# Rotary embedding on one core: tile 3's load moves from SyncE's queue to GpSimd's and waits for tile 1's arithmetic

## The chip, the core and the metric

One core of one Trainium2 chip. The metric is the device time of one execution in microseconds (us), as the median of several runs. Engines that matter here: VectorE (DVE), which does all the arithmetic; SyncE (SP) and GpSimd (POOL), which issue transfers from their queues; and the core's 16 DMA engines, which carry the transfers out. TensorE and ScalarE are not used.

## The reference

Half of each head's 64 elements are rotated in pairs by position, the other half is passed through:

```python
batch, seq, heads, dim = (16, 512, 16, 64)
x1, x2 = x[..., :32], x[..., 32:]
rotated_first  = x1[..., :16] * cos[..., :16] - x1[..., 16:] * sin[..., :16]
rotated_second = x1[..., :16] * sin[..., :16] + x1[..., 16:] * cos[..., :16]
out = concatenate([rotated_first, rotated_second, x2], axis=-1)   # float32
```

`x` has 16 x 512 x 16 x 64 float32 numbers, 33.55 MB, and the output has as many. `cos` and `sin` (512 x 32) are small; their first 16 columns are used.

## The kernel before

The 8192 rows of `x` (batch and position; one row is 16 heads of 64, 4 KB) are cut into four tiles, t = 0 to 3. A tile has 128 partitions with 16 consecutive rows each: 64 KB on a partition, 8.39 MB in all. The tiles lie in `ring`, which has three slots (`NS = 3`), so tile 3 uses tile 0's slot again. Work is in place: a tile is loaded into its slot, half of each head is rotated there, and the whole slot is stored from there. So tile 3 can be loaded only when tile 0 has been stored.

`load` (line 56) and `store` (line 59) each issue one DMA for the rows lo to hi of a tile. `rotate` (lines 91 to 112) does a tile or a part of one with four kinds of instruction on VectorE: two multiplications (lines 97 and 98, the first into a PSUM buffer `b_t`, the second in place), a subtraction (line 99) and an addition (line 106). It returns the subtraction and the list of additions, so that a transfer can be tied to one of them. `hold` (lines 114 to 122) ties it: the transfer is issued only after that instruction has ended. The framework adds the waits that the data need by itself: a load into a used slot waits for the landing of that slot's stores, a store waits for the arithmetic on its rows, and the arithmetic waits for its load's landing.

The table of cosines and sines is made first (lines 62 to 89): two small DMAs from GpSimd's queue (lines 64 and 65) and some copies on VectorE. Tiles 0 and 1 and the upper half of tile 2 are loaded meanwhile (lines 66 to 68).

The main part (lines 124 to 141) gives the order of issue on each queue. Each queue works its own list in order, and an entry that waits holds up what is behind it:

- SP: loads of tile 0, tile 1 and the upper half of tile 2; the two stores of tile 0 (lines 126 and 127; the first is held until the third quarter of tile 0 is done); load of the lower half of tile 2 (line 128); load of tile 3 (line 129); store of tile 1 (line 132, held by line 138 until the subtraction of rows 0 to 4 of tile 2); store of tile 3 (line 141).
- POOL: the two table loads, then the store of tile 2 (line 136).
- DVE: tile 0 in two halves, tile 1 in two halves, tile 2's upper half, then its rows 0 to 4, then 5 to 7, then tile 3 in two halves.

Of the kernel before, what the change touches and what calls it, by code (L numbers as in the profile page):

```python
# [1 line left out]

# [4 lines left out]


@with_exitstack
def kernel(  # L10
    ctx: ExitStack,
    tc: tile.TileContext,
    x: bass.AP,
    cos: bass.AP,
    sin: bass.AP,
    out: bass.AP,
):
    nc = tc.nc
    fp32 = mybir.dt.float32
    P = 128  # L20
    B, S, H, D = x.shape
    Q = D // 4
    HF = D // 2

    K = 16
    T = B * S // (P * K)
    PB = S // K
    REP = P // PB  # L30
    R = H * D
    NS = 3
    KC = K // 2
    KM = 5
    KP = K - 4

    xf = x.rearrange("b s h d -> (b s h d)").rearrange("(t p f) -> t p f", t=T, p=P)
    of = out.rearrange("b s h d -> (b s h d)").rearrange("(t p f) -> t p f", t=T, p=P)
    cosf = cos.rearrange("(p k) j -> p (k j)", k=K)
    sinf = sin.rearrange("(p k) j -> p (k j)", k=K)  # L40

    const_pool = ctx.enter_context(tc.tile_pool(name="const", bufs=1))
    b_pool = ctx.enter_context(tc.tile_pool(name="bp", bufs=1, space=bass.MemoryType.PSUM))


    ring = const_pool.tile([P, NS, K, H, D], fp32)
    stage = const_pool.tile([P, 2, K, HF], fp32)
    spun = const_pool.tile([P, 2 * K, Q], fp32)
    packed = const_pool.tile([PB, 2 * K, Q], fp32)
    table = const_pool.tile([P, 2, K, 2, Q], fp32)  # L50

    def rows(t, lo, hi):
        return ring[:, t % NS, lo:hi].rearrange("p k h d -> p (k h d)")

    def load(t, lo=0, hi=K):
        return nc.sync.dma_start(out=rows(t, lo, hi), in_=xf[t, :, lo * R : hi * R])

    def store(t, lo=0, hi=K, queue=nc.sync):
        return queue.dma_start(out=of[t, :, lo * R : hi * R], in_=rows(t, lo, hi))  # L59


    nc.vector.memset(stage[:, :, :, 0:Q], 0.0)  # L62
    spread = stage.rearrange("(j b) t k i -> j b t (k i)", b=REP)
    nc.gpsimd.dma_start(out=spread[:, 0, 0], in_=cosf)  # L64
    nc.gpsimd.dma_start(out=spread[:, 0, 1], in_=sinf)  # L65
    load(0)
    load(1)
    load(2, KC, K)

    PQ = PB // REP
    nc.vector.stream_shuffle(  # L74
        out=spun[:],
        in_=stage.rearrange("p t k j -> p (t k) j")[:, :, 0:Q],
        mask=[j % PQ * REP for j in range(PB)],
    )
    for q in reversed(range(REP)):
        n = PQ * (q + 1)  # L80
        nc.vector.tensor_copy(out=packed[0:n], in_=spun[q * PB : q * PB + n])  # L81

    for r in range(REP):
        nc.vector.tensor_copy(  # L84
            out=table[r * PB : (r + 1) * PB].rearrange("p t k c j -> p (t k) c j"),
            in_=packed.unsqueeze(2).to_broadcast((PB, 2 * K, 2, Q)),
        )
    C = table[:, 0].rearrange("p k c j -> p k (c j)")
    Sn = table[:, 1].rearrange("p k c j -> p k (c j)")

    def rotate(t, lo, hi, cut=None):
        x1 = ring[:, t % NS, lo:hi, :, 0:HF]
        c = C[:, lo:hi].unsqueeze(2).to_broadcast((P, hi - lo, H, HF))
        s = Sn[:, lo:hi].unsqueeze(2).to_broadcast((P, hi - lo, H, HF))
        b_full = b_pool.tile([P, KC, H, HF], fp32, name="b_t")
        b_t = b_full[:, 0 : hi - lo]
        nc.vector.tensor_mul(out=b_t, in0=x1, in1=s)  # L97
        nc.vector.tensor_mul(out=x1, in0=x1, in1=c)  # L98
        first = nc.vector.tensor_sub(  # L99
            out=x1[:, :, :, 0:Q], in0=x1[:, :, :, 0:Q], in1=b_t[:, :, :, Q:HF]  # L100
        )
        ends = [hi - lo] if cut is None else [cut - lo, hi - lo]
        done = []
        for a, b in zip([0] + ends, ends):
            done.append(
                nc.vector.tensor_add(  # L106
                    out=x1[:, a:b, :, Q:HF],
                    in0=x1[:, a:b, :, Q:HF],
                    in1=b_t[:, a:b, :, 0:Q],
                )  # L110
            )
        return first, done

    def hold(transfer, point):
        tc.add_manual_dep(
            transfer.ins,
            point.ins.name,
            mybir.DependencyInfo(
                mybir.DependencyClass.Sync, mybir.DependencyReason.DATA
            ),  # L120
            reason="the store follows the loads at the DMA engines",
        )

    rotate(0, 0, KC)
    _, close = rotate(0, KC, K, cut=KP)
    hold(store(0, 0, KC), close[0])
    store(0, KC, K)
    load(2, 0, KC)
    load(3)
    rotate(1, 0, KC)  # L130
    rotate(1, KC, K)
    behind_loads = store(1)
    rotate(2, KC, K)
    near, _ = rotate(2, 0, KM)
    rotate(2, KM, KC)
    store(2, queue=nc.gpsimd)

    hold(behind_loads, near)
    rotate(3, 0, KC)
    rotate(3, KC, K)  # L140
    store(3)


# [1 line left out]
_INS = ['x', 'cos', 'sin']  # L145
_OUTS = [((16, 512, 16, 64), 'float32')]


# [23 lines left out]
```

## Time and profile before

| what | us |
|---|---|
| median of 3 runs (lowest to highest) | 161.62 (161.36 to 161.76) |
| the profiled execution's own time | 161.67 |
| its span (first to last instruction of the program) | 159.8 |
| VectorE busy | 113.0 (71%) in 48 instructions |
| GpSimd busy | 1.9 (1%) in 7 instructions |
| data moved by the DMA engines | 67.24 MB, 421 GB/s over the span |

The profile counts microseconds from the start of the span; 1.87 us of the profiled execution's time lie outside it. It tells for each engine when its instructions ran and what they waited for. For the DMA engines it has a record of each packet, with its queue, start, duration and size: q1 is SP's queue, q0 is POOL's. A packet of a tile's transfer is one partition's piece, 64 KB for a whole tile and 32 KB for half a tile, and each of the 16 engines carries the pieces of 8 partitions. In its tables over windows of time a packet's whole time and size are booked where the packet starts, so that a window's DMA share can be over 1.

### The profile page before, as it was taken

The page shows a single profiled execution, that of the slowest core. Times are in us where ns is not written, and L with a number is a line of the kernel's source. Part 1 is how long each engine was busy: PE and PEld are TensorE (multiplying, and loading weights), DVE is VectorE, ACT ScalarE, POOL GpSimd, SP SyncE. Part 2 cuts the span into 40 slices and gives each one's busy share as a digit, 9 for nine tenths or more (in the row PEclk, how much of TensorE's full clock was granted, in tenths as well). Part 3 has the DMA queues.
Part 4 walks back from the last instruction along what each step waited for, and adds up shares of the span by engine and source line. Part 5 has one row for each costly group of instructions (what it writes and reads, how often), then busy time and mean ns, then how long its engine had stood idle before and what let it go on. Part 6 is the DMA issues. An engine that isn't in the chain of part 4 may idle for free.

```text
span 159.8 us, 120 instructions
## 1 busy us (share of the span) xinstructions
DVE 113.0 (71%) x48; POOL 1.9 (1%) x7
## 2 busy tenths in 40 slices
DVE  1000959999999999999999999999999980000000
POOL 3000000000000000000000000010000000000000
DMA  7969989899799999999999799996996996996990
GB/s 262 541 262 541 410 377 525 377 410 525 303 467 410 394 484 426 402 402 508 402 525 476 312 525 394 394 525 295 492 525 262 525 508 279 525 508 279 525 508 16
DMA packets 1504, 67.24 MB, mean 421 GB/s; under 512 B 192, under 2 KB 192, under 8 KB 224
## 3 DMA queue, kind: packets, MB, share of 16 engines
q1 hardware_dynamic: 1296, 58.72, 85.4%
q0 software_dynamic: 208, 8.52, 12.3%
HBM read 33.69 MB, written 33.55 MB: 421 GB/s over the span
## 4 chain that ended last, share of the span: by engine, by line
DVE 61%; DMA 14%; issue 5%; DVEq 1%
DVE b_t L97 22%; DVE ring L98 22%; DMA ring<-in_x_dram 14%; DVE ring L106 10%; DVE ring L99 7%; DVEq L167 1%; DVEq L97 0%
## 5 line engine op out<-in xcount | busy, mean ns | idle before, releaser
L97 DVE TENSOR_TENSOR b_t<-ring,table 128x4096 f32<-128x4096 f32 (+2 forms) x9 | 35.6, 3958 | 2.1 <-DMA ring<-in_x_dram 1.9
L98 DVE TENSOR_TENSOR ring<-ring,table 128x4096 f32<-128x4096 f32 (+2 forms) x9 | 35.6, 3950 | 0.3
L99 DVE TENSOR_TENSOR ring<-ring,b_t 128x2048 f32<-128x2048 f32 (+2 forms) x9 | 18.4, 2050 | 0.3
L106 DVE TENSOR_TENSOR ring<-ring,b_t 128x2048 f32<-128x2048 f32 (+3 forms) x10 | 18.4, 1853 | 0.0
L74 DVE LOAD_MASK_SELECT spun<-stage x1 | 0.0, 14 | 14.4 <-DMA stage<-in_sin_dram 14.4
L84 DVE COPY table<-packed 32x1024 f32<-32x1024 f32 x4 | 2.7, 684 | 0.1
L59 POOL DMA_DIRECT2D out_dram<-ring x1 | 0.6, 562 | 101.8 <-DVE ring L106 101.8
L81 DVE COPY packed<-spun 32x512 f32<-32x512 f32 (+3 forms) x4 | 1.7, 416 | 0.1
L62 DVE MEMSET stage<- 128x512 f32 x1 | 0.5, 485 | 0.9 <-PEq L156 0.9
L74 DVE STREAM_SHUFFLE spun<-stage 128x512 f32<-128x512 f32 x1 | 0.7, 721 | 0.0
L64 POOL DMA_DIRECT2D stage<-in_cos_dram x1 | 0.6, 644 | 1.3 <-DVE stage L62 1.3
L65 POOL DMA_DIRECT2D stage<-in_sin_dram x1 | 0.5, 535 | 0.0
L156 POOL MEMSET const-bfloat16-1.0<- 128x1 bf16 x1 | 0.1, 102 | 0.0
L156 POOL MEMSET const-float32-0.0<- 128x1 f32 x1 | 0.1, 99 | 0.2 <-issue 0.2
L156 POOL MEMSET const-float32-1.0<- 128x1 f32 x1 | 0.1, 99 | 0.0
L156 POOL MEMSET const-uint8-127<- 128x1 uint8 x1 | 0.1, 99 | 0.0
## 6 DMA issues: line engine op xcount, KB each, us to landing
ring<-in_x_dram SPq DMA_DIRECT2D x2, 4096.0 KB, 40.8
out_dram<-ring SPq DMA_DIRECT2D x2, 4096.0 KB, 17.4
stage<-in_cos_dram POOLq DMA_DIRECT2D x1, 64.0 KB, 9.0
stage<-in_sin_dram POOLq DMA_DIRECT2D x1, 64.0 KB, 13.4
ring<-in_x_dram SPq DMA_DIRECT2D x3, 28.9
out_dram<-ring SPq DMA_DIRECT2D x2, 31.1
out_dram<-ring POOLq DMA_DIRECT2D x1, 39.6
```

Of the source, the lines that this page charges most:

```text
L59: return queue.dma_start(out=of[t, :, lo * R : hi * R], in_=rows(t, lo, hi))
L62: nc.vector.memset(stage[:, :, :, 0:Q], 0.0)
L64: nc.gpsimd.dma_start(out=spread[:, 0, 0], in_=cosf)
L65: nc.gpsimd.dma_start(out=spread[:, 0, 1], in_=sinf)
L74: nc.vector.stream_shuffle(out=spun[:], in_=stage.rearrange("p t k j -> p (t k) j")[:, :, 0:Q], mask=[j % PQ * REP for j in range(PB)],)
L81: nc.vector.tensor_copy(out=packed[0:n], in_=spun[q * PB : q * PB + n])
L84: nc.vector.tensor_copy(out=table[r * PB : (r + 1) * PB].rearrange("p t k c j -> p (t k) c j"), in_=packed.unsqueeze(2).to_broadcast((PB, ...
L97: nc.vector.tensor_mul(out=b_t, in0=x1, in1=s)
L98: nc.vector.tensor_mul(out=x1, in0=x1, in1=c)
L99: first = nc.vector.tensor_sub(out=x1[:, :, :, 0:Q], in0=x1[:, :, :, 0:Q], in1=b_t[:, :, :, Q:HF])
L106: nc.vector.tensor_add(out=x1[:, a:b, :, Q:HF], in0=x1[:, a:b, :, Q:HF], in1=b_t[:, a:b, :, 0:Q],)
L167: with _tile.TileContext(nc) as tc:
```

## The change

The load of tile 3 gets two new properties. It is issued from GpSimd's queue, ahead of the store of tile 2 there, and no longer from SyncE's, where it stood ahead of the store of tile 1. And it is held until the last addition of tile 1 has ended, beside the wait for the landing of tile 0's stores that it keeps. Sizes, tiles and arithmetic are the same.

```diff
-    def load(t, lo=0, hi=K):
-        return nc.sync.dma_start(out=rows(t, lo, hi), in_=xf[t, :, lo * R : hi * R])
+    def load(t, lo=0, hi=K, queue=nc.sync):
+        return queue.dma_start(out=rows(t, lo, hi), in_=xf[t, :, lo * R : hi * R])
...
     load(2, 0, KC)
-    load(3)
+    behind_load = load(3, queue=nc.gpsimd)
     rotate(1, 0, KC)
-    rotate(1, KC, K)
+    _, close = rotate(1, KC, K)
+    hold(behind_load, close[0])
     behind_loads = store(1)
```

## The prediction

> **What bounds the kernel.** The chain of waits ends in DVE (61% of the span), but DVE's last instruction ends at 131.3 us (L106 starts at 129.01, lasts 2.28) and the span at 159.8: the last 28 us are only a transfer. So I read the DMA side: the page's slices and queues.
>
> ```profile
> DMA  7969989899799999999999799996996996996990
> DMA packets 1504, 67.24 MB, mean 421 GB/s; under 512 B 192, under 2 KB 192, under 8 KB 224
> q1 hardware_dynamic: 1296, 58.72, 85.4%
> q0 software_dynamic: 208, 8.52, 12.3%
> ```
>
> The two shares add to 97.7% of 16 engines' span. The digits of 6 or 7 are an effect of booking a packet where it starts. To see whether anything is idle I chained the packet records by engine (each packet's start to the end of the one before): every one of the 16 engines runs from 1.74–2.84 us to 157.8–158.5 us with no gap over 0.1 us. A 64 KB packet takes 2.418 us on q1 and on q0, for loads and for stores (a few on q1 take up to 3.5, most of them the first), and a 32 KB packet 1.21. Per engine 64 such 64 KB (4.19 MB) make 64 x 2.418 = 154.8 us. **The DMA engines are the bound, full from the first packet to the last.** So no reordering can gain; a change can only lose, by leaving an engine without a packet. Every other delay costs nothing as long as a queue has work.
>
> **Where the moved load stands now.** The timeline around it:
>
> ```profile
> 67.93 4.42 DVE L98 TENSOR_TENSOR ring<-ring,table 128x4096 f32<-128x4096 f32 x1
> 71.91 0.34 SPq L56 DMA_DIRECT2D ring<-in_x_dram  x1
> 72.39 2.29 DVE L99 TENSOR_TENSOR ring<-ring,b_t 128x2048 f32<-128x2048 f32 x1
> 74.59 2.28 DVE L106 TENSOR_TENSOR ring<-ring,b_t 128x2048 f32<-128x2048 f32 x1
> 76.91 4.43 DVE L97 TENSOR_TENSOR b_t<-ring,table 128x4096 f32<-128x4096 f32 x1
> ```
>
> SP issues it at 71.91, when tile 0's second store has landed. The packet records say what it meets: the lower half of tile 2 is under way, its last 32 KB packets start at 79.28–79.74 and end at 80.49–80.96 (fastest and slowest engine), and tile 3's first packets start in the same hundredth. It has been in the queue 8.6 us by then. That is the cover of the delay: the load can be issued later at no cost while its first packet is ready at 80.5 on the fastest engine, 80.96 on the slowest. The slowest is the one that counts: it also ends 0.4 us after nearly all the others (158.45 against 157.8–158.0), so a common stop of the others up to 0.4 us is free.
>
> **The change part by part.**
>
> *Issue.* SP loses one issue of 0.34 us, in a queue that otherwise waits (20.1 us ahead of this load, 25.3 ahead of tile 1's store). Behind it on SP stands tile 1's store, still held until the subtraction that ends at 97.57 (96.08 + 1.49): it goes out at 97.59 as before. Gain nothing. POOL gets one issue, of about 0.56 us by its own row below, in a queue that slept 101.8 us; behind the waiting load on POOL stands only tile 2's store, due at 104.71, long after the load is out. Cost nothing.
>
> *Wait.* Tile 1's last addition ends at 74.59 + 2.28 = 76.87. How long then until packets flow? The nearest row is POOL's own store of tile 2, released in the same way by the same kind of instruction:
>
> ```profile
> 103.46 0.94 DVE L106 TENSOR_TENSOR ring<-ring,b_t 128x768 f32<-128x768 f32 x1
> 104.44 4.43 DVE L97 TENSOR_TENSOR b_t<-ring,table 128x4096 f32<-128x4096 f32 x1
> 104.71 0.56 POOL L59 DMA_DIRECT2D out_dram<-ring  x1 [101.82 <-DVE ring L106]
> ```
>
> Addition end (104.40) to POOL issue: 0.30 us, so load 3 is issued at 77.17. From the store's issue to its first q0 packet 4.84 us pass (109.54 on four engines; 111.9–112.1 on the other twelve), but the engines were busy with q1: a packet is chosen some time before it starts. Two bounds follow.
>
> Lower: if an engine chooses its next packet when the present one starts (107.05–107.73 for those engines), the store was visible at about 107.1–107.3, 2.4–2.6 us after issue. SP's store of tile 3 speaks for this lead: issued at 131.32, not taken at the 133.6 boundary by any engine, though the idle engines at the start took SP's first load 1.0 us after issue (0.74 to 1.74). So the lead is over 133.6 − 132.3 = 1.3 us. Then load 3 is visible at 77.17 + 2.4 to 2.6 = 79.6–79.8; with the least lead, 1.3 us, at 77.17 + 3.5 = 80.7. An engine that had run dry would pay 0.5–1.1 us more on its first packet (2.9–3.5 against 2.42 at the start); I take 0.7. On the slowest engine: 79.7 + 0.7 = 80.4 against 80.96: nothing lost. At the least lead: 80.7 + 0.7 − 80.96 = 0.4 us lost.
>
> Upper: no lead at all, a full 4.84 us from issue: first packet at 82.01, loss 82.01 − 80.96 = 1.05 us, with the 0.7 of a cold start 1.75 us. Below nothing it can't go: no engine has a gap to give back.
>
> I take the lead of one packet, since the SP row excludes a lead near nothing: **cost 0, with 0 to 1.75 as ends.**
>
> One rule could speak against the change. The POOL store was issued inside a multiplication with two SBUF inputs (L97, 104.44–108.87), as load 3 would be (76.91–81.34), and its issue took 562 ns against 644 and 535 of the two table loads, issued with DVE idle; so the row shows no block at the issue, though the first packets came only after that multiplication's end. The Trainium skill, SBUF — State Buffer, "SBUF: two separate sides", says that DVE in a two-port mode locks GpSimd out of the shared port and that descriptors can't be written until the DVE instruction ends plus about 115 ns; for two SBUF inputs it limits this to GpSimd work that reads SBUF. An estimate by the strict reading puts the descriptors at 81.34 + 0.12 = 81.46, a loss of 0.5 us without a cold start; by the limited reading there is none.
>
> *After the load's start.* Load 3 has q0 to itself beside q1's rest of tile 2, which ends first. Its 8 packets per engine then run alone, to 80.5 + 8 x 2.418 = 99.8, as before. Tile 1's store (97.59) is visible at 98.6 at the earliest; if load 3 started late, the engines would alternate, and its last packet or its closing semaphore would come one packet (2.42) later, landing at 103.2 instead of 100.8. DVE needs it at 104.44. Beyond that DVE has a reserve of its own: tile 2's store leaves q0 with packets until 140.9 once tile 3's store is held back, so that store, issued at 131.32, could go out some 7 us later (140.9 − 2.3 − 131.3) before an engine is idle. So 2.4 us on landing cost nothing, and the order of packets from 98 us on can't move the end.
>
> *Sum.* Own time of the profiled execution 161.67 (span 159.8 + 1.87) + 0 = 161.7, beside a median of 161.62.
>
> **Rivals.**
>
> *Slower: the software queue is too slow for the cover.* If load 3's first packet comes more than 80.96 − 77.17 = 3.8 us after POOL's issue, every engine stops between tile 2's last packet and it, and the end moves by as much, since no slack lies behind it. Price 0.5 to 1.75 us: 162.2 to 163.4, centre 162.8. For it: 4.84 us are what the one 64 KB row on q0 shows at face value, and the multiplication beside it is the same. Against it: those engines were never idle, and SP's row shows that a choice is made at least 1.3 us ahead.
>
> *No change, but DVE pays.* Load 3 lands late behind alternating packets and DVE waits at 104.44 for up to some 2 us. The 7 us of reserve swallow it: 161.7. It would need over 7 us to decide otherwise.
>
> *The wait does not act.* Suppose the load went out at tile 0's landing as before, from POOL: visible about 74.4, it would alternate 64 KB packets with tile 2's remaining four or five of 32 KB, which would land 9.7 to 12.1 us later, at 91–93.5 against DVE's need at 90.35. DVE late by 1 to 3 us, still inside the 7: 161.7. The issue time on POOL tells this case apart.
>
> *Faster.* Only stretched packets could give: about 0.3 us each where tile 2's upper half gives way to tile 0's store (50 us) and where that gives way to tile 2's lower half (69.3 us, 1.5–1.6 instead of 1.21). The change touches neither; 161.1 at the very best.
>
> **Chances.** What a measurement of this kernel can tell from no change is about 0.3%, 0.48 us. Hidden (with DVE late or not, with the wait or without): 0.55, 161.7. Packets too late: 0.40, 162.2–163.4; the sum excludes it only by a lead that is inferred, so it keeps much weight. Faster: 0.05. The range goes from 161.2, a little under the lowest run of before, to 163.4, the upper bound of the wait.
>
> **What would show it.** Right: POOL's issue at about 77.2; q0's first 64 KB packets within 80.5–81.0 and no engine with a gap; the load's landing at about 101; DVE without a wait ahead of 104.44; tile 3's store landing at 158–159. Wrong: an issue well after 77.2, a dip of the DMA share in the slice at 80–84 us, the last landing later by the same amount as the dip. If q0's packets of a load took more than 2.418 us each, the loss would be spread over 80–100 us, and my assumption that loads cost the same on both queues would be what failed.

## The result and the profile after

The changed kernel takes 162.16 us (median of 9 runs, 161.92 to 162.60) against 161.54 for the kernel before, run beside it (9 runs, 161.36 to 161.88): ratio 1.0038, 95% interval 1.0027 to 1.0050. That is 0.62 us, just over the 0.48 us that the prediction took as what a measurement can tell. The two profiled executions, 161.67 and 162.10, differ by 0.43.

First the moved load. Of the changed kernel, the timeline around its issue (start, duration, engine, line, operation; in brackets how long the engine sat idle before and for whom):

```profile
74.60 2.28 DVE L106 TENSOR_TENSOR ring<-ring,b_t 128x2048 f32<-128x2048 f32 x1
76.92 4.43 DVE L97 TENSOR_TENSOR b_t<-ring,table 128x4096 f32<-128x4096 f32 x1
77.18 0.55 POOL L56 DMA_DIRECT2D ring<-in_x_dram  x1 [74.30 <-DVE ring L106]
```

It is issued at 77.18 by GpSimd, 0.30 us after tile 1's last addition. The windows of the changed kernel after that (busy time of DVE and POOL, clock, DMA share, GB/s) show no window in which packets are missing:

```profile
78.00:80.00 2.00, 2.00 (x1) 0.00 (x0) 1.00 1.14 492
80.00:82.00 2.00, 1.97 (x2) 0.00 (x0) 1.00 1.21 524
82.00:84.00 2.00, 2.00 (x1) 0.00 (x0) 1.00 1.21 524
```

The packet records agree: the load's first packets start at 80.34 to 80.82 on q0, 0.01 us after tile 2's last ones on q1, and take 2.418 us. Chained by engine, no engine has a gap over 0.05 us in the whole execution. And yet they end at 158.5 to 159.0 instead of 157.8 to 158.5. So packets must have become longer. Windows around the end of the load, of the kernel before:

```profile
96.00:99.00 3.00, 2.93 (x4) 0.00 (x0) 1.00 0.81 350
99.00:101.50 2.50, 2.47 (x2) 0.00 (x0) 1.00 0.97 419
101.50:104.00 2.50, 2.47 (x3) 0.00 (x0) 1.00 0.97 419
```

and of the changed kernel:

```profile
96.00:99.00 3.00, 2.94 (x3) 0.00 (x0) 1.00 0.81 350
99.00:101.50 2.50, 2.46 (x2) 0.00 (x0) 1.00 1.28 419
101.50:104.00 2.50, 2.46 (x3) 0.00 (x0) 1.00 0.97 419
```

Each window holds one packet per engine, booked where it starts: 96 to 99 the last packets of tile 3's load, 99 to 101.5 the first packets of tile 1's store. The last two columns are the point: the same bytes (419 GB/s), but a share of 1.28 instead of 0.97. The difference, 0.31 x 2.5 us = 0.78 us per engine, is the loss. The records say the same of single packets (three packets in a row of one engine of the changed kernel: queue, start, duration, bytes):

```
q0 97.24 2.42 65536      last packet of tile 3's load
q1 99.66 3.28 65536      first packet of tile 1's store
q1 102.94 2.42 65536
```

All 16 first packets of the store take 3.07 to 3.32 us instead of 2.42; everything after is as fast as before, only later. The store is issued where it was (first the kernel before, then the changed one):

```profile
97.59 0.34 SPq L59 DMA_DIRECT2D out_dram<-ring  x1
97.60 0.33 SPq L59 DMA_DIRECT2D out_dram<-ring  x1
```

So the changed kernel loses nothing where the load moved to, and 0.7 to 0.8 us where the store takes over from it. What differs there is that load and store were in one queue (q1) and are now in two.

The same two traces show what does not cost. A load that follows a load of the other queue has packets of normal length: the changed kernel at 80.34. So has a store that joins a store of the other queue, on full engines and from a queue that had been idle: in the kernel before, the first packets of tile 2's store, from 109.54 on, and of tile 3's, from 136.03 on, all take 2.42 us. So neither a change of queues nor an idle queue is dear in itself; what is left is a store that follows a load of the other queue.

### The profile page after: what moved, and what is told of

It reads as the page before. It is cut to its first block, busy times and chain, and to the rows that moved or that the text cites. A ratio compares the mean times of both kernels' runs of the same rounds, so it can differ in the third digit from the quotient of the medians.

```text
span 160.3 us, 121 instructions
## 1 busy us (share of the span) xinstructions
DVE 113.0 (70%) x48; POOL 2.5 (2%) x8
## 4 chain that ended last, share of the span: by engine, by line
DVE 61%; DMA 14%; issue 5%; DVEq 1%
DVE b_t L97 22%; DVE ring L98 22%; DMA ring<-in_x_dram 14%; DVE ring L106 10%; DVE ring L99 7%; DVEq L168 1%; DVEq L97 0%
## 5 line engine op out<-in xcount | busy, mean ns | idle before, releaser
L56 POOL DMA_DIRECT2D ring<-in_x_dram x1 | 0.6, 551 | 74.3 <-DVE ring L106 74.3
```

The source lines that it names most:

```text
L56: return queue.dma_start(out=rows(t, lo, hi), in_=xf[t, :, lo * R : hi * R])
```

## The experiments

Below, "handover" is the point near 100 us where the load of tile 3 ends and the store of tile 1 begins, and times are medians beside runs of the kernel before on the same chip (161.47 to 161.55).

**1. The wait alone** (against the changed kernel):

```diff
-    behind_load = load(3, queue=nc.gpsimd)
+    behind_load = load(3)
```

> The load of tile 3 stays on SP's queue and only waits for the end of tile 1's arithmetic. In the changed kernel nothing is lost at that load's start (its first packets follow tile 2's last ones without a gap); the loss of 0.6 to 0.8 us is in the first packets of tile 1's store, 3.07 to 3.32 us instead of 2.42, the first store packets to follow load packets of another queue. Theory 'two queues' (T1 and T2 below are its kinds): with both transfers in one queue the first store packets take 2.42 us and the time is that of before, 161.5. Rival 'the wait costs': about 162.2, with the loss at the load's start near 80 us. Load issued at 76.9.

Measured: 161.44, ratio 0.9998 (0.9986 to 1.0009). Its windows:

```profile
96.00:99.00 3.00, 2.97 (x3) 0.00 (x0) 1.00 0.83 350
99.00:101.50 2.50, 2.43 (x3) 0.00 (x0) 1.00 0.97 419
```

The load is issued at 76.95, which costs nothing; the first store packets take 2.42 us. The wait is free, and the loss belongs to the queue. One thing shows in the share of 0.83: on the two latest engines the load's last packets, which start at 97.72 and 97.92, just after the store's issue at 97.64, take 2.73 and 3.07 us. The profiled execution, one of the slower ones (162.16), ends 0.5 us later on its last engine than the kernel before (158.95 against 158.44).

**2. The store sooner** (against the changed kernel; `second` is the multiplication of line 98, returned by `rotate` as a third value):

```diff
-    near, _ = rotate(2, 0, KM)
+    _, _, near = rotate(2, 0, KM)
```

> The changed kernel, but tile 1's store is held to the end of the second multiplication of tile 2's rows 0 to 4 (96.06) instead of the subtraction (97.57), so it is issued 1.5 us sooner, at about 96.1, and reaches the engines at about 97.1, ahead of the start of the load's last packets (97.24 to 97.72) instead of in the midst of them. Theory T1, a late joiner: the queue of the store was empty and its first packet was not prepared in time, so sooner arrival removes the 0.8 us: 161.5, first store packets 2.42 us. Theory T2, a change from load to store between two queues costs 0.8 us whatever the arrival: 162.2, first store packets still 3.1 to 3.3 us.

Measured: 162.45, ratio 1.0054 (1.0042 to 1.0066). The store is issued at 96.21. Windows:

```profile
96.00:99.00 3.00, 2.97 (x3) 0.00 (x0) 1.00 1.04 350
99.00:101.50 2.50, 2.43 (x3) 0.00 (x0) 1.00 0.97 419
```

T1 falls: sooner is no cure. T2's time is nearly met, but not its packets: now the load's last packets are stretched (2.74 to 3.66 us) and the store's first ones are not.

**3. ScalarE's queue in place of GpSimd's:**

```diff
-    behind_load = load(3, queue=nc.gpsimd)
+    behind_load = load(3, queue=nc.scalar)
```

> The changed kernel with the load of tile 3 on ScalarE's queue instead of GpSimd's, with the same wait. Theory T3, the software queue is the cause: a hardware queue in its place gives 161.5 and first store packets of 2.42 us. T1 and T2: two queues remain, the store joins as late as before, 162.2 and 3.1 to 3.3 us.

Measured: 162.35, ratio 1.0050 (1.0038 to 1.0062). Windows:

```profile
96.00:99.00 3.00, 2.97 (x3) 0.00 (x0) 1.00 0.83 350
99.00:101.50 2.50, 2.43 (x3) 0.00 (x0) 1.00 1.26 419
```

14 of the first store packets take 3.07 to 3.31 us, and on the two late engines last load packets of 3.04 and 3.12 with first store packets of 2.73 and 2.79. The software queue is not the cause (T3 falls).

**4. The queue alone:**

```diff
-    hold(behind_load, close[0])
```

> The changed kernel without the added wait: the load goes to GpSimd's queue as soon as tile 0's stores have landed (about 72). Its 64 KB packets then alternate with the last four or five 32 KB packets of tile 2, which land at about 91 to 93 instead of 81, and VectorE, which needs them at 90.35, is 1 to 3 us late. The record's own statement was that the 7 us reserve at the end swallows that: 161.7. Against it: tile 1's store hangs on that arithmetic, is issued as much later, and the load is done at 99.8, so that from a delay of some 1.2 us on the engines run dry before the store comes: 163 to 165, with a gap at about 100 us.

Measured: 162.13, ratio 1.0040 (1.0026 to 1.0055). The load goes out at 72.39 and its packets do alternate with tile 2's, which land at 91.0 instead of 81.4. VectorE waits for that:

```profile
91.11 2.83 DVE L97 TENSOR_TENSOR b_t<-ring,table 128x2560 f32<-128x2560 f32 x1 [0.67 <-DMA ring<-in_x_dram]
98.35 0.33 SPq L59 DMA_DIRECT2D out_dram<-ring  x1
```

It is 0.67 us late, not 1 to 3, and the store still comes before the load has ended, so no engine runs dry (is left without a packet). Both figures I gave fail: 161.7 as it left out the handover (0.87 us of stretch here), 163 to 165 as the delay was smaller. The wait that the change adds is worth nothing in time here.

**5. The load's last rows back on SP's queue:**

```diff
-    behind_load = load(3, queue=nc.gpsimd)
+    behind_load = load(3, 0, KP, queue=nc.gpsimd)
+    last_load = load(3, KP, K)
...
-    rotate(2, KC, K)
+    _, close = rotate(2, KC, K)
+    hold(last_load, close[0])
```

> The changed kernel, but the last four of the load's sixteen rows per partition go out from SP's queue, held to the end of the arithmetic on tile 2's upper half (90.3), ahead of tile 1's store there. SP's queue, empty since 81, thus starts again with a load, and the store follows in a queue that is at work. Theory T5, a queue that has run empty pays some 0.7 us when it starts again: the loss stays, 162.2, and moves to about 92 us. Theory T2, the loss belongs to a store in one queue that follows loads in another: it goes or becomes small, 161.5 to 161.6, no stretched packets at 92 us and first store packets near 2.42 us.

Measured: 161.77, ratio 1.0022 (1.0007 to 1.0038). From 60 us on no packet is stretched but four at 69.6 to 69.8, by 0.09 to 0.15 us each; SP's queue starts again at 95.0 with packets of normal length, so T5 falls. The 0.2 us above the kernel before are not at the handover. The profiled execution has longer packets from 46 to 52 us, by 0.31 us per engine against 0.06 in the kernel before; what causes them there is open.

**6. Both on the software queue, the store sooner** (against run 2):

```diff
-    behind_loads = store(1)
+    behind_loads = store(1, queue=nc.gpsimd)
```

> The changed kernel with tile 1's store on GpSimd's queue too, behind the load, and held to the second multiplication of tile 2's rows 0 to 4 (so that GpSimd's later start, 2.4 to 2.6 us after the issue at about 96.3, still falls within the load's last packets, which end at 99.7 to 100.4). Load and store are in one queue again, the software one. Both T2 and T5: first store packets 2.42 us and 161.5. If GpSimd's start were later than reckoned, gaps at about 100 us and up to 1 us more would show.

Measured: 162.19, ratio 1.0037 (1.0025 to 1.0049): a miss for both theories. Load and store are in one queue, and the load's last packets take 2.88 to 3.85 us. The store was issued at 96.25, and as in run 2 that is before the last load packets began (97.33 to 97.81). So one queue alone is not enough. By run 8's start of 1.25 to 1.9 us the store would be there at 97.5 to 98.2, after most of those packets began; so what counts seems to be the issue rather than such an arrival.

**7. Loads beside stores in another place** (against the kernel before, with the `queue` argument that `load` has in the changed kernel; `close` is that of tile 0):

```diff
-    load(2, 0, KC)
+    hold(load(2, 0, KC, queue=nc.scalar), close[0])
```

> The kernel before, but the load of tile 2's lower half goes out from ScalarE's queue, held to the third quarter of tile 0 (48.9), so that its 32 KB load packets alternate with the 32 KB store packets of tile 0 in SP's queue. By arithmetic alone tile 0's stores end at about 80 instead of 71, the load of tile 3 can't be issued before, and the engines stop for some 2.5 us at 80 to 83: 164. On top of that T2 in its strict form, every handover from a load to a store of another queue costs 0.7 us, would add 0.7 for each of 8 to 16 alternations, 170 to 175; in its mild form (once, when the store joins) 0.7, 164.7; T5 (a restarted queue) nothing at 50 us.

Measured: 165.09, ratio 1.0218 (1.0192 to 1.0243). Here 8 load and 8 store packets per engine alternate from 52 to 71 us on two queues, and every one of them takes 1.21 us; only the packets of 48 to 52 us, where the two transfers join, are longer, by 0.29 us per engine in all. So alternating is not dear, and strict T2 falls. The stop at 80 to 83 (1.8 us on average) comes, if shorter than the 2.5 reckoned, followed by 0.67 us of longer first packets of a load on dry engines. And at the handover, with both transfers on SP's queue but one more load packet per engine still to begin after the store is issued (97.62), the last load packets take 3.35 to 4.00 us, a loss of 1.3.

**8. The load held to the next instruction of VectorE** (`late` is the multiplication of line 97, returned by `rotate` as a third value):

```diff
-    hold(behind_load, close[0])
...
-    rotate(2, KC, K)
+    _, _, late = rotate(2, KC, K)
+    hold(behind_load, late)
```

> The changed kernel with the load held to the next instruction of VectorE, the first multiplication of tile 2's upper half (ends at 81.35) instead of tile 1's last addition (76.9): issued at about 81.65, when the engines have run dry at 80.3 to 80.8. It measures the price of a start that nothing covers. By the prediction's reckoning the load is visible 2.4 to 2.6 us after issue, 84.1 to 84.3, plus 0.7 of a cold start, so a stop of 3.3 to 3.9 us and 0.7 stretched; the load then ends at about 104, after the store of tile 1 has joined, so that the later handover changes too: 165.5 to 166.5. If a software start took only about 1 us: 164 to 165.

Measured: 165.65, ratio 1.0251 (1.0234 to 1.0268). The issue, with what VectorE does at the time, and the windows of this run:

```profile
81.42 4.42 DVE L98 TENSOR_TENSOR ring<-ring,table 128x4096 f32<-128x4096 f32 x1
81.69 0.55 POOL L56 DMA_DIRECT2D ring<-in_x_dram  x1 [78.80 <-DMA ring<-in_x_dram]
```

```profile
80.00:82.00 2.00, 1.97 (x2) 0.31 (x1) 1.00 0.00 0
82.00:84.00 2.00, 2.00 (x1) 0.24 (x1) 1.00 1.59 524
```

No packet starts between 80 and 82. The first ones start at 82.94 to 83.61, so a software start takes 1.25 to 1.9 us from issue on dry engines, not 2.4 to 2.6. The time fell in the expected range by a sum of other parts: a stop of 2.6 us on average, 0.76 us of longer first packets (share 1.59 against 1.21), and 1.08 us at the handover, where the store is issued before the last load packets begin.

**9. The kernel before, the store sooner:** run 2's edit on the kernel before, both transfers on SP's queue.

> The kernel before, tile 3's load and tile 1's store both on SP's queue, but the store held to the second multiplication of tile 2's rows 0 to 4 (issued at about 96.1 instead of 97.6), so that it arrives before the load's last packets start. In the runs so far the stretch also came with both transfers in one queue when the store arrived that soon (0.71 us on the software queue, 1.3 us on SP's after a late load). Theory TB, the arrival counts (a store known before the last load packet begins stretches that packet, in any queue): 162.2 to 162.8, last load packets 2.8 to 3.8 us. Theory TA, only two queues cost: 161.5, all packets 2.42 us.

Measured: 162.64, ratio 1.0061 (1.0039 to 1.0083), with the change nowhere in it:

```profile
96.00:99.00 3.00, 2.97 (x3) 0.00 (x0) 1.00 1.07 350
99.00:101.50 2.50, 2.43 (x3) 0.00 (x0) 1.00 0.91 393
```

TB's figures hold: with the store issued at 96.19, before the last load packets begin, these take 2.77 to 3.73 us in one queue too, 0.26 x 3 = 0.78 us more per engine on average. The last engine ends 1.15 us later (159.59 against 158.44), and it decides the time.

**10. Both on the software queue, the store as held before** (against the changed kernel; run 6's edit without run 2's):

> The changed kernel with tile 1's store behind the load on GpSimd's queue, held to the subtraction as before (issued at about 97.9; a software start on dry engines took 1.25 us at the least, so it arrives at 99.1 or later, within the load's last packets, which end at 99.7 to 100.4). TA: one queue, no loss, 161.5, first store packets 2.42 us. TB: arrival within the last packets, no loss, 161.5. If the software queue itself hands over badly: 0.7 us, 162.2, as in the run with the sooner store.

Measured: 161.25, ratio 0.9977 (0.9961 to 0.9992). Store issued at 98.09:

```profile
96.00:99.00 3.00, 2.96 (x3) 0.54 (x1) 1.00 0.81 350
99.00:101.50 2.50, 2.43 (x3) 0.00 (x0) 1.00 0.97 419
```

One edit to the changed kernel, the store put into the queue of the load, takes the whole loss away. It also issues the store 0.49 us later (98.09 against 97.60), so this run alone would not tell the queue from the time; runs 1 and 12, with the store at 97.64 and 97.65, do. It is even 0.2 us under the kernel before, the only version whose interval lies below it; what that last bit is, its profile does not show (engines end at 157.7 to 158.4, as before).

**11. The store later** (against the changed kernel; held to the addition after the subtraction):

```diff
-    near, _ = rotate(2, 0, KM)
+    _, near = rotate(2, 0, KM)
...
-    hold(behind_loads, near)
+    hold(behind_loads, near[0])
```

> The changed kernel with tile 1's store held to the addition of tile 2's rows 0 to 4 (ends at 98.98) instead of the subtraction, so it reaches SP's empty queue at about 100.0, when the load's packets end (99.7 to 100.4). Does a store in another queue cost its 0.7 to 0.8 us however late it comes? If the stretch is a cold start that the switch of queues pays in any case: stretched first packets and a gap of up to 0.3 us, 162.3 to 162.6. If it comes only from an overlap with the load's last packets: first packets of 2.42 us after a gap of 0.1 to 0.4, 161.6 to 161.9.

Measured: 162.04, ratio 1.0027 (1.0014 to 1.0041), between the two forecasts, so that the packets have to decide:

```profile
99.00:101.50 2.50, 2.43 (x3) 0.00 (x0) 1.00 0.99 419
```

The store is issued at 99.33; its first packets start at 100.16 and after and take 2.44 to 2.47 us, after a gap of 0.39 us on average. A store on dry engines has no cold start to speak of; the loss is now mostly the gap. So the first packets of 3.2 us in the changed kernel are no price of switching queues as such; they come when the store joins while the load is still under way.

**12. The kernel before, only the store on another queue:**

```diff
-    behind_loads = store(1)
+    behind_loads = store(1, queue=nc.scalar)
```

> The kernel before with nothing changed but the queue of tile 1's store: ScalarE's instead of SP's, with the same hold (issued at about 97.6). The load of tile 3 stays on SP's queue at 71.9. TA, two queues at this arrival cost 0.7 to 0.8 us: 162.2, first store packets 3.1 to 3.3 us, as in the changed kernel, with the load untouched. If what counted in the changed kernel was the moved load itself: 161.5.

Measured: 162.20, ratio 1.0037 (1.0024 to 1.0051). Its windows:

```profile
96.00:99.00 3.00, 2.96 (x3) 0.00 (x0) 1.00 0.81 350
99.00:101.50 2.50, 2.43 (x3) 0.00 (x0) 1.00 1.29 419
```

The first store packets take 3.08 to 3.31 us: the changed kernel's loss, with the load untouched in its queue and at its time. The store is issued at 97.65, 0.06 us later than in the kernel before, so the queue is all that differs. TA's figures hold. TA and TB do not exclude each other: a store issued at this time costs only in another queue, and one issued 1.4 us sooner costs in one queue too.

## Why the prediction was partly right

- *The bound.* Right: the DMA engines are full throughout in both kernels, and every microsecond lost there is lost at the end. The conclusion drawn from it was wrong: "So no reordering can gain; a change can only lose, by leaving an engine without a packet." The loss came with no engine idle: packets took longer.
- *Issue and wait.* Right in the outcome: issue at 77.2 as reckoned, first packets at 80.34 to 80.82, cost 0 (run 1 and run 10). The reason was too cautious: the software start takes 1.25 to 1.9 us (run 8), so the load was ready at about 78.4 to 79.1 rather than 79.6 to 79.8, if full engines see it as soon as dry ones. Tile 2's store, issued at 104.71 and first carried at 109.54, was then most likely late since the full engines had other packets chosen, and not because VectorE blocked its issue: SP's store of tile 3 needed as long on full engines, from 131.32 to 136.03. The cold start of 0.7 us that the prediction took fits loads on dry engines (0.67 to 0.76, runs 7 and 8) but not a store (run 11).
- On that, the Trainium skill's page SBUF — State Buffer, "SBUF: two separate sides", has GpSimd shut out until VectorE's instruction ends if VectorE is in a two-port mode, and for two SBUF inputs only from reading. Run 8 agrees with the limited reading: issued within a multiplication with two SBUF inputs (81.42 to 85.84), its packets flow from 82.94.
- *After the load's start.* This is the step that failed: "the order of packets from 98 us on can't move the end". It counted packets and their order at a fixed 2.418 us each. The handover from the load's queue to the store's costs 0.78 us (after against before; runs 3 and 12 repeat it, runs 1 and 10 remove it). The landing itself was harmless, as said: 100.65 instead of 100.79, with VectorE at 104.45 as before.
- *The rivals.* "Slower" came true at the lower end of its price (162.2), but not by its mechanism or at its place: nothing stops at 80 us. That 162.16 lies within the range of 161.2 to 163.4 is luck: the part of the range above 161.7 was priced by a stop that did not happen, and the cost that came in its place happened to lie near its smallest figure, 0.5. "The wait does not act" was priced 161.7 and measures 162.13 (run 4), for the same handover.
- *The sum.* 161.7 left out one term, 0 instead of 0.78, of which 0.43 show between the two profiled executions and 0.62 between the medians: the first engine ends 0.7 us later than in the kernel before (158.5 against 157.8), the last one 0.5 (159.0 against 158.5), and the last one counts.

Put together, the runs bound the handover from three sides. A store issued before the last load packets begin stretches those, by 0.7 to 1.3 us per engine, in one queue or two (runs 2, 6, 7, 8, 9). The border lies close to the issue: in the kernel before, with the store issued at 97.59, the last load packets of 15 engines start at 97.39 to 97.66 and take 2.42 us, that of the 16th starts at 97.89 and takes 2.60; run 1's two latest engines agree. A store issued when the last load packets have just begun is free in the same queue (before, runs 1 and 10, the latest engines apart) and costs 0.7 to 0.9 in another (after, runs 3, 4, 12). One that comes when the load has ended leaves a gap of its own (run 11). Run 5 does not fit: the store was issued at 97.61, well before its last load packets began (99.2 to 99.8; they are 16 KB and take 0.61 us), and nothing was stretched. Whether the size of the packets or the time that is left decides there is open. What an engine does in the lost 0.7 us, no record shows; that stays open too.

## What to carry to other kernels

What follows is shown for this kernel alone, with full DMA engines and packets of 64 KB. Where the DMA engines bound a kernel, "no idle engine" is only half of the reading: compare the duration of packets too, by windows with equal bytes and unequal DMA share, above all where loads hand over to stores. Keep the last load and the store that follows it in one queue, and let the store be issued when the last load packets have just begun, neither sooner nor later. Moving a transfer to another queue changes the neighbours of transfers that were not touched.

## What the runs showed of the hardware that was not expected

- Issuing a load and the next store from two queues cost 0.7 to 0.8 us on every engine (in the changed kernel first store packets of 3.07 to 3.32 us instead of 2.42), with hardware queues as with the software one. Load after load, and store beside store, of two queues cost nothing (80.34 in the changed kernel, 109.54 and 136.03 in the kernel before). The Trainium skill's page DMA: Bandwidth & Descriptors, "Issuing engines are not separate DMA queues", says that transfers of several issuing engines interleave on the same 16 engines and that using several saves only issue time; runs 3, 4 and 12 show that it can also cost.
- A store issued 1.4 us too soon, in the unchanged arrangement, cost 1.2 us (162.64 against 161.47, ratio 1.0061).
- First packets of a load on dry engines took 0.67 to 0.76 us more (runs 7 and 8); those of a store on dry engines 0.02 to 0.05 (run 11).
- Load and store packets of 32 KB that alternated between two queues from 52 to 71 us were not stretched at all (run 7).
